# More sevens in the feed-forward blocks, and four first tiles side by side, in a two-layer hybrid model on one core

## The chip, the core and the metric

The kernel runs on 1 core of one Trainium2 chip. The metric is the device time of one execution in microseconds, the median of several runs. Everything is fp32 at the interface; the kernel must return the reference's result for one sequence of 256 tokens with 2048 features.

## What is computed

Two layers. The first mixes tokens by a gated delta rule (8 heads) and a gated linear recurrence, the second by two kinds of softmax attention (8 heads each). After each mixer stands a feed-forward block (SwiGLU), and each of the four parts adds to the residual h:

```python
D_MODEL, SEQ, DEPTH = 2048, 256, 2
D_FF = 5632

def rmsnorm(x, w):
    return x * rsqrt(mean(x * x, axis=-1, keepdims=True) + 1e-6) * w

def swiglu(hn, w_gate, w_up, w_down):
    return (silu(hn @ w_gate) * (hn @ w_up)) @ w_down

h = x
for layer in range(DEPTH):
    if layer % 2 == 0:
        h = h + gdn_rglru_mixer(rmsnorm(h, ab_norm), ...)      # projections, recurrences, w_out
    else:
        h = h + fox_moba_mixer(rmsnorm(h, cd_norm), ...)       # projections, attention, w_out
    h = h + swiglu(rmsnorm(h, ffn_norm[layer]), w_gate[layer], w_up[layer], w_down[layer])
return rmsnorm(h, final_norm)
```

## The kernel before

**Exact products from a fast format.** Every weight tile comes from HBM as fp32 (`raw`, 128 x 1024). ScalarE rounds it to the fast matmul format (`hi`, `S.copy`), VectorE subtracts (`lo = raw - hi`): function `split`. Activations are held the same way, as a pair in `X` or `hid`. A product is then three matmuls: x_hi by w_hi, x_hi by w_lo, x_lo by w_hi. So each weight tile costs a DMA of 512 KB, a cast on ScalarE, a subtraction on VectorE, and matmuls.

**Stages.** `mixer0`, `ffn(0)`, `mixer1`, `ffn(1)` run one after the other, each mixer and each feed-forward part as a phase with tile pools of its own (`phase`). Pools in a feed-forward phase: `hid` (the hidden pair, one buffer), `fx` (everything else, reached as `mx`). The pools for weights lie outside the phases: `wr` (3 buffers, raw), `wh` (4, hi), `wl` (3, lo); in a feed-forward phase four more raw buffers (`raw4`) take four of every seven loads. PSUM has two pools of four banks: `acc` and `msp` (tiles by `ms`).

**Feed-forward.** `ffn` cuts the 5632 hidden features into 11 blocks of 512, in pieces of 4, 4 and 3. A gate/up block (`block` with 4 groups) multiplies X with 512 columns of w_gate and of w_up; both have 2048 rows, four groups of 512. After a piece, two down blocks multiply its `hid` with w_down (4 or 3 groups each) and add to h. In `block`, a plain group is four weight tiles, each for both halves of the tokens: 48 matmuls of 512 columns. A group in `comb` is taken by sevens, as in Strassen's scheme: the 2 x 2 products of (token halves) x (tile pairs) are made from seven products of sums. `combine` makes the sums of the activations (`comb`, on VectorE and ScalarE), `total` those of the weights: a sum T on VectorE, its cast thi on ScalarE, its remainder tlo on VectorE. Seven products of 6 matmuls make 42. `ends` joins the four extra banks M with the banks F: four VectorE operations and a copy on ScalarE, and where F is used (SiLU and product, or adding to h) four more VectorE operations take part. `seven` yields after each product, and `block` deals these steps out between the plain tiles from tile `lead` on. Which groups go by sevens is set in `ffn`: in gate/up block b it is one for b = 0 and for odd b, else two; in a down block always one (`ch`, combined from hid).

`turn` transposes a finished block's activations into `hid` (4 matmuls, a copy, a subtraction); it runs as a hook ahead of a numbered tile of the next block, one half of the tokens at a time, at tiles 2 and 3. Other hooks make `combine(X...)`, `rstd` (the norm's factor, from sums of squares in `ssp`) and `combine(hid...)`.

**The start of mixer0.** `first` (L205) brings xt, the transposed input, in four quarters of 4 k (128 features each), and with each quarter half of three weight tiles; for each it makes X (ScalarE, VectorE), the splits, and 3 tiles x 4 k x 3 matmuls of 256 columns. Then `wstat` takes the other tiles one by one (two loads of 128 x 1024 each, 16 matmuls of 512 columns by hi, 16 of 256 by lo), into a bank of `acc`. Six matmuls on zeros (`Pz`) run ahead. After the first of these tiles, x is loaded into h in four parts, and `sumsq` squares it on ScalarE with a sum; `rstd` follows, and `rstd_rows` after the second tile spreads it over rows (`Prb`). Every finished tile waits for that in its bank, and `convs` then works on two for each new tile.

Each engine works its own list in order; the order between engines comes from semaphores. All loads are issued by SP, in order. Small pieces of the mixers' work are generators, `start`ed and stepped by `tick` after each weight tile.

Of the kernel before, what the change touches and what calls it, by code (L numbers as in the profile page):

```python
# [5 lines left out]
AF = mybir.ActivationFunctionType  # L6
# [4 lines left out]
D = 2048  # L11
# [25 lines left out]
NTAB0 = 152  # L37
# [10 lines left out]
def body(tc, A, out):  # L48
# [13 lines left out]
    mx, ogp = Phase(), Phase()  # L62
# [26 lines left out]
    for _ in range(6):  # L89
        PE.matmul(Pz, wz[:, 128:256], wz[:, 0:256], start=True, stop=True)  # L90
# [91 lines left out]
    def wstat(src, wide=False, mid=None):  # L182
# [5 lines left out]
        P = acc.tile([128, n, T], F32, name="Pw", tag="acc")  # L188
# [16 lines left out]
    def first(srcs, w):  # L205

        xt = ogp.tile([128, NK, T], F32, name="xt", tag="og")
        Ps = [ms([128, T], "Pw") for _ in srcs]
        for q in range(4):
            ks, c = slice(4 * q, 4 * q + 4), slice(q % 2 * 512, q % 2 * 512 + 512)  # L210
            nc.sync.dma_start(xt[:, ks], A["xt"][:, ks])
            if q % 2 == 0:
                ws = [(wr.tile([128, 1024], F32, name="raw"), wh.tile([128, 1024], F32R, name="whi"),
                       wl.tile([128, 1024], F32R, name="wlo")) for _ in srcs]
            for i, (raw, _, _) in enumerate(ws):
                nc.sync.dma_start(raw[:, c], srcs[i][q // 2][:, c])
            if q == 0:
                nc.sync.dma_start(tab[:, 0:NTAB0], A["tab"][:, 0:NTAB0])
                nc.sync.dma_start(col[:, 16:], A["col"][:, 16:])
            for k in range(4 * q, 4 * q + 4):  # L220
# [3 lines left out]
            for P, (raw, hi, lo) in zip(Ps, ws):  # L224
# [3 lines left out]
                for k in range(4 * q, 4 * q + 4):  # L228
# [3 lines left out]
        return Ps  # L232
# [63 lines left out]
    def rstd():  # L296
# [3 lines left out]
        V.tensor_reduce(out=x, in_=ssp, axis=AX.X, op=ALU.add)  # L300
        V.tensor_scalar(out=x, in0=x, scalar1=1.0 / D, scalar2=EPS, op0=ALU.mult, op1=ALU.add)
# [33 lines left out]
    def total(a, b, name):  # L335
# [3 lines left out]
        hi = mx.tile([128, 1024], F32R, name="thi", tag="thi", bufs=2)  # L339
        lo = mx.tile([128, 1024], F32R, name="tlo", tag="tlo", bufs=2)  # L340
# [4 lines left out]
    def combine(x4):  # L345
# [3 lines left out]
        r = mx.tile([128, 2, 4, 2, 128], F32R, name="comb", tag="comb", bufs=3)  # L349
# [22 lines left out]
    def block(src, x, comb, nd, hooks, tail=0, lead=2):  # L372
# [9 lines left out]
        M = [Bank(ms([128, 512], f"M{j}"), ns) for j in range(4)]  # L382
# [62 lines left out]
    def ffn(L, then, fin=None):  # L445
# [4 lines left out]
        def turn():  # L450
            hid, j, t, a = todo.pop(0)
            P = ms([128, 4, 128], "Ph")
            for i in range(4):
                PE.transpose(P[:, i], a[:, i * 128:(i + 1) * 128], tb["ident"])  # L454
            d = hid[:, 4 * j:4 * j + 4, :, t * 128:(t + 1) * 128]
            S.copy(d[:, :, 0], P)
            V.tensor_tensor(out=d[:, :, 1], in0=P, in1=d[:, :, 0].bitcast(F32), op=ALU.subtract)

        b = 0
        for piece in (4, 4, 3):  # L460
            hid = ogp.tile([128, 16, 2, T], F32R, name="hid", tag="hid")
            for j in range(piece):
                hooks = {2: turn, 3: turn} if todo else {}
                if b == 0:
                    hooks[4] = lambda: cx.update({0: combine(X[:, 0:4])})
                    hooks[8] = rstd
                if j == (3 if piece == 4 else 1):
                    hooks[5] = lambda: ch.update({0: combine(hid[:, 0:4])})
                if b == 1:
                    hooks[8] = lambda: cx.update({1: combine(X[:, 4:8])})  # L470
                F, e = block(lambda i, u: gu[b, u, i], lambda k: X[:, k],
# [720 lines left out]
```

## Time and profile before

| | us |
|---|---|
| median of 3 runs | 2254.43 (2252.94 to 2254.56) |
| the profiled execution | 2252.67 |
| its span, first to last instruction | 2250.8 |
| granted TensorE clock | 0.999 |
| TensorE busy in the span | 2232.4 (99%) |
| VectorE busy | 1881.8 (84%) |
| ScalarE busy | 1253.1 (56%) |
| first feed-forward part, first to last matmul | 437.2 to about 1138 |
| second one | 1539.5 to 2241 |

PE is TensorE, PEld its weight loads, DVE VectorE, ACT ScalarE, SP the engine that issues the loads. A row of a group gives the busy time, the mean of one in ns, the idle time of its engine just ahead of it and what ended it. A row of waits names the waiting engine and line, then what it waited for: us in total, times, the longest.

### The profile page before, as it was taken

What the parts mean: (1) busy time and instruction counts of PE and PEld (TensorE: products, weight loads), DVE (VectorE), ACT (ScalarE), POOL (GpSimd) and SP (SyncE); (2) the same over time, 40 slices, a digit from 0 to 9 for tenths busy, and PEclk for the clock granted to TensorE, in tenths of its full rate; (3) what the DMA queues carried; (4) which work ended last, traced back from release to release, by engine and by line L of the source; (5) the groups of instructions that cost most, each with busy time, mean ns of one, the idle gap of its engine ahead of it and who ended that gap; (6) DMA issues with size and microseconds to landing.
All of it is one profiled execution on the core that took longest, in us unless ns stands there. A gap on an engine that the chain in (4) does not pass through costs nothing.

```text
span 2250.8 us, 30139 instructions
## 1 busy us (share of the span) xinstructions
PE 2232.4 (99%) x11070; PEld 1862.6 (83%) x11070; DVE 1881.8 (84%) x2681; ACT 1253.1 (56%) x1663; POOL 2.0 (0%) x6
## 2 busy tenths in 40 slices
PE   8999999999999999999999999999999999999998
PEld 7888888888888888888878888887888888888886
DVE  7899676699979998899976658858998898988998
ACT  7876764565545554455644444445565455555564
POOL 0000000000000000000000000000000000000000
PEclk9999999999999999999999999999999999999999
DMA  7454455666666666666555455556666666566563
GB/s 254 143 175 153 145 155 179 209 211 196 204 199 197 200 193 196 202 199 203 172 153 169 150 170 176 165 184 213 204 196 197 202 205 203 189 202 206 193 218 122
DMA packets 118643, 422.29 MB, mean 188 GB/s; under 512 B 13248, under 2 KB 14784, under 8 KB 118368
## 3 DMA queue, kind: packets, MB, share of 16 engines
q1 hardware_dynamic: 118208, 419.84, 58.7%
q8 instruction: 87, 1.43, 0.3%
q14 instruction: 60, 0.49, 0.1%
q10 hardware_dynamic: 288, 0.52, 0.1%
HBM read 418.22 MB, written 2.10 MB: 187 GB/s over the span
## 4 chain that ended last, share of the span: by engine, by line
PE 95%; DVE 2%; DMA 2%; ACT 0%; issue 0%; SPq 0%; DVEq 0%; ACTq 0%
PE F L368 17%; PE F L369 17%; PE F L367 17%; PE Pw L194 11%; PE Pw L199 5%; PE Px L268 4%; PE Px L269 4%; PE Px L270 4%; PE M L368 4%; PE M L369 4%; PE M L367 3%; PE Ph L454 1%; DMA raw<-in_w0w 1%; DVE wlo L175 1%; PE Psc L997 1%; PE Pt L291 0%
## 5 line engine op out<-in xcount | busy, mean ns | idle before, releaser
L174 ACT CAST whi<-raw 128x1024 fp32r<-128x1024 f32 x734 | 770.9, 1051 | 752.5 <-PE F L369 360.7
L175 DVE TENSOR_TENSOR wlo<-raw,whi 128x1024 fp32r<-128x1024 f32 x734 | 890.2, 1221 | 208.6 <-PE Px L269 67.2
L194 PE MATMUL Pw<-X,whi 128*128 128x512 f32 x1104 | 397.0, 402 | 0.9 <-ACT whi L174 0.9
L367 PE MATMUL F<-whi,X 128*128 128x512 f32 x960 | 375.8, 392 | 0.0
L368 PE MATMUL F<-wlo,X 128*128 128x512 f32 x960 | 374.1, 390 | 0.3 <-DVE wlo L175 0.3
L369 PE MATMUL F<-whi,X 128*128 128x512 f32 x960 | 373.7, 389 | 0.0
L199 PE MATMUL Pw<-X,wlo 128*128 128x256 f32 x1104 | 309.1, 280 | 2.1 <-DVE wlo L175 2.1
L342 DVE TENSOR_TENSOR tlo<-T,thi 128x1024 fp32r<-128x1024 f32 x176 | 214.5, 1222 | 44.2 <-ACT thi L341 43.6
L194 PEld LDWEIGHTS Pw<-X,whi 128*128 128x128 f32 x1104 | 207.2, 188 | 49.9 <-ACT whi L174 1.1
L341 ACT CAST thi<-T 128x1024 fp32r<-128x1024 f32 x176 | 185.1, 1052 | 103.8 <-DVE T L338 80.0
L368 PEld LDWEIGHTS F<-wlo,X 128*128 128x128 f32 x960 | 180.3, 188 | 37.6 <-DVE wlo L175 1.2
L369 PEld LDWEIGHTS F<-whi,X 128*128 128x128 f32 x960 | 180.2, 188 | 37.6
L199 PEld LDWEIGHTS Pw<-X,wlo 128*128 128x128 f32 x1104 | 208.4, 189 | 3.3 <-DVE wlo L175 2.8
L367 PEld LDWEIGHTS F<-whi,X 128*128 128x128 f32 x960 | 180.2, 188 | 36.6
L367 PE MATMUL F<-whi,hid 128*128 128x512 f32 x536 | 209.9, 392 | 0.0
L369 PE MATMUL F<-whi,hid 128*128 128x512 f32 x536 | 208.8, 390 | 0.0
L368 PE MATMUL F<-wlo,hid 128*128 128x512 f32 x536 | 208.7, 389 | 0.0
L369 PEld LDWEIGHTS F<-whi,hid 128*128 128x128 f32 x536 | 100.6, 188 | 21.0
L368 PEld LDWEIGHTS F<-wlo,hid 128*128 128x128 f32 x536 | 100.7, 188 | 20.5
L367 PEld LDWEIGHTS F<-whi,hid 128*128 128x128 f32 x536 | 100.6, 188 | 20.4
L338 DVE TENSOR_TENSOR T<-raw,raw 128x1024 f32<-128x1024 f32 x74 | 90.4, 1223 | 28.0 <-DMA raw<-in_dn 19.0
L338 DVE TENSOR_TENSOR T<-T,raw 128x1024 f32<-128x1024 f32 x88 | 107.5, 1222 | 3.8 <-DMA raw<-in_dn 3.3
(371 smaller groups left out, 3126.2 us busy)
## 6 DMA issues: line engine op xcount, KB each, us to landing
raw<-in_gu SPq DMA_DIRECT2D x352, 512.0 KB, 4.0
raw<-in_dn SPq DMA_DIRECT2D x176, 512.0 KB, 4.2
raw<-in_w0w SPq DMA_DIRECT2D x74, 512.0 KB, 3.7
raw<-in_wo SPq DMA_DIRECT2D x64, 512.0 KB, 3.6
raw<-in_w1w SPq DMA_DIRECT2D x64, 512.0 KB, 3.6
raw<-in_w1x SPq DMA_DIRECT2D x32, 512.0 KB, 3.7
raw<-in_w0x SPq DMA_DIRECT2D x16, 512.0 KB, 3.6
raw<-in_w0w SPq DMA_DIRECT2D x12, 256.0 KB, 5.2
```

The source lines that it names most:

```text
L174: S.copy(hi, raw)
L175: V.tensor_sub(lo, raw, hi.bitcast(F32))
L194: PE.matmul(P.rearrange("p a b -> p (a b)"), hi[:, kk], X[:, k].rearrange("p a b -> p (a b)"), start=k == 0, stop=False)
L199: PE.matmul(P[:, 0], lo[:, kk], X[:, k, 0], start=False, stop=k == NK - 1)
L268: PE.matmul(Ps[t], x[:, 0, ts], hi[:, kk], start=k == 0, stop=False)
L269: PE.matmul(Ps[t], x[:, 0, ts], lo[:, kk], start=False, stop=False)
L338: V.tensor_tensor(out=t, in0=a, in1=b, op=ALU.add)
L341: S.copy(hi, t)
L342: V.tensor_sub(lo, t, hi.bitcast(F32))
L367: PE.matmul(self.t, xh, hi[:, kk], start=self.i == kk == 0, stop=False)
L368: PE.matmul(self.t, xh, lo[:, kk], start=False, stop=False)
L369: PE.matmul(self.t, xl, hi[:, kk], start=False, stop=kk == 1 and self.i == self.n - 1)
```

## The change

1. In `ffn`, the number of groups by sevens is written out for each gate/up block: 0, 2, 2, 2 in the first piece, 2, 2, 2, 2 in the second, 2, 2, 2 in the third. Down blocks keep one. A block without sevens has no M banks and no `ends`; its F go straight to SiLU and product. `combine(hid)` moves from the last gate/up block of a piece to the first down block after it, whose `lead` becomes 5; in the last piece it stays in the second gate/up block. `combine(X...)` is done twice in the first block (tiles 5 and 10).
2. `turn` takes both halves at one hook (tile 2): eight transposes, then the copies and subtractions.
3. A pool `fp` of its own, in the feed-forward phases, for thi, tlo, comb and fa.
4. `first` takes four tiles in pieces of 2, 2, 4, 4 and 4 k, into `acc`; the fourth tile's raw lies in h and `rawb`, its lo in `lob`. The squares are taken in place in xt, and the task `squares` adds them and sums them over features by two one-column matmuls; `rstd` takes the result from PSUM. x is loaded into h behind the ninth to twelfth of the following tiles in the program; in the order of SP's list its four loads stand behind the third, sixth, seventh and ninth weight load that follows `first`. The next three tiles go to `msp` (`spare`). The first load of tables is 280 columns instead of 152, and `Pz` has five matmuls.

The diff, cut to its core:

```diff
-NTAB0 = 152
+NTAB0 = 280
...
+        if not mixer:
+
+            fp.pool = sub("fp", 1)
...
-    for _ in range(6):
+    for _ in range(5):
...
-    def wstat(src, wide=False, mid=None):
+    def wstat(src, wide=False, mid=None, spare=False):
...
-        P = acc.tile([128, n, T], F32, name="Pw", tag="acc")
+        P = ms([128, n, T], "Pw") if spare else acc.tile([128, n, T], F32, name="Pw", tag="acc")
...
     def first(srcs, w):
         xt = ogp.tile([128, NK, T], F32, name="xt", tag="og")
-        Ps = [ms([128, T], "Pw") for _ in srcs]
-        for q in range(4):
-            ks, c = slice(4 * q, 4 * q + 4), slice(q % 2 * 512, q % 2 * 512 + 512)
+        rawb = ogp.tile([128, 4, 1024], F32, name="rawb", tag="og")
+        lob = ogp.tile([128, 4, 1024], F32R, name="lob", tag="og")
+        Ps = [acc.tile([128, T], F32, name="Pw", tag="acc") for _ in srcs]
+        for k0, k1 in ((0, 2), (2, 4), (4, 8), (8, 12), (12, 16)):
+            v, ks, c = k0 // 8, slice(k0, k1), slice(k0 % 8 * 128, k0 % 8 * 128 + (k1 - k0) * 128)
             nc.sync.dma_start(xt[:, ks], A["xt"][:, ks])
...
+            if k0 == 0:
+                raws = [wr.tile([128, 1024], F32, name="raw") for _ in range(3)] + [h[:, 1, 0:1024]]
+            elif k0 == 8:
+                raws = [rawb[:, i] for i in range(4)]
+            if k0 % 8 == 0:
+                his = [wh.tile([128, 1024], F32R, name="whi") for _ in srcs]
+                los = [wl.tile([128, 1024], F32R, name="wlo") for _ in range(3)] + [lob[:, v]]
+            for raw, src in zip(raws, srcs):
+                nc.sync.dma_start(raw[:, c], src[v][:, c])
...
+            if k0 % 4 == 0 and k1 > 2:
+                S.activation(xt[:, ks], xt[:, ks], AF.Square)
+            elif k0 == 2:
+                S.activation(xt[:, 0:4], xt[:, 0:4], AF.Square)
+        return Ps, xt
+
+    def squares(sq):
+        add = lambda a, b: V.tensor_tensor(out=sq[:, a], in0=sq[:, a], in1=sq[:, b], op=ALU.add)
+        add(slice(0, 4), slice(4, 8))
+        add(slice(8, 12), slice(12, 16))
+        yield
+        for a, n in ((8, 4), (2, 2), (1, 1)):
+            add(slice(0, n), slice(a, a + n))
+        yield
+        P = ms([128, 2], "Prs")
+        for t in range(2):
+            PE.matmul(P[:, t:t + 1], sq[:, 0, t * 128:(t + 1) * 128], tb["ones"][:, 0:1], start=True, stop=True)
+        rstd(P)
...
-        hi = mx.tile([128, 1024], F32R, name="thi", tag="thi", bufs=2)
-        lo = mx.tile([128, 1024], F32R, name="tlo", tag="tlo", bufs=2)
+        hi = fp.tile([128, 1024], F32R, name="thi", tag="thi", bufs=2)
+        lo = fp.tile([128, 1024], F32R, name="tlo", tag="tlo", bufs=2)
...
-        for piece in (4, 4, 3):
+        for groups in ((0, 2, 2, 2), (2, 2, 2, 2), (2, 2, 2)):
+            piece = len(groups)
             hid = ogp.tile([128, 16, 2, T], F32R, name="hid", tag="hid")
+            late = {4: lambda hid=hid: ch.update({0: combine(hid[:, 0:4])})}
             for j in range(piece):
-                hooks = {2: turn, 3: turn} if todo else {}
+                hooks = {2: turn} if todo else {}
                 if b == 0:
-                    hooks[4] = lambda: cx.update({0: combine(X[:, 0:4])})
+                    hooks[5] = lambda: cx.update({0: combine(X[:, 0:4])})
                     hooks[8] = rstd
-                if j == (3 if piece == 4 else 1):
-                    hooks[5] = lambda: ch.update({0: combine(hid[:, 0:4])})
-                if b == 1:
-                    hooks[8] = lambda: cx.update({1: combine(X[:, 4:8])})
-                F, e = block(lambda i, u: gu[b, u, i], lambda k: X[:, k],
-                             {m: lambda m=m: cx[m] for m in range(2 - b % 2 if b else 1)}, 4, hooks, lead=2 if b else 5)
+                    hooks[10] = lambda: cx.update({1: combine(X[:, 4:8])})
+                if j == 1 and piece == 3:
+                    hooks.update(late)
+                F, e = block(lambda i, u: gu[b, u, i], lambda k: X[:, k], {m: lambda m=m: cx[m] for m in range(groups[j])}, 4, hooks)
...
-                             {2: turn, 3: turn} if todo else {}, 3 if end and fin else 0)
+                hooks = {2: turn} if todo else {}
+                if p == 0 and piece == 4:
+                    hooks.update(late)
+                F, e = block(lambda i, u: dn[2 * p + i, u0 + u], lambda k: hid[:, k], {0: lambda: ch[0]}, piece, hooks,
+                             3 if end and fin else 0, 5 if 4 in hooks else 2)
...
-        for n, o in enumerate(order[3:]):
-            waiting.append((*o, wstat(tile_of(*o), True, mid=ready if n == 1 else None)))
+        start(squares(sq), 1)
+        for n, o in enumerate(order[4:]):
+            waiting.append((*o, wstat(tile_of(*o), True, mid=ready if n == 1 else None, spare=n < 3)))
             if n == 0:
-                for g in range(4):
-                    nc.sync.dma_start(h[:, :, g * 512:(g + 1) * 512], A["x"][:, :, g * 512:(g + 1) * 512])
-                    sumsq(g)
                 nc.sync.dma_start(tab[:, NTAB0:], A["tab"][:, NTAB0:])
-                rstd()
                 start(lru_rate())
                 continue
+            if n >= 8 and n < 12:
+
+                nc.sync.dma_start(h[:, :, (n - 8) * 512:(n - 7) * 512], A["x"][:, :, (n - 8) * 512:(n - 7) * 512])
```

More of the change, by code (lines that the diff above doesn't have):

```diff
@@ L223, in first @@
                                        op0=ALU.mult, op1=ALU.subtract)
-            for P, (raw, hi, lo) in zip(Ps, ws):
+            for P, raw, hi, lo in zip(Ps, raws, his, los):
                 S.copy(hi[:, c], raw[:, c])
@@ L227, in first @@
                 hi, lo = (t.rearrange("p (k n) -> p k n", n=128) for t in (hi, lo))
-                for k in range(4 * q, 4 * q + 4):
+                for k in range(k0, k1):
                     PE.matmul(P, hi[:, k % 8], X[:, k, 0], start=k == 0, stop=False)
@@ L381, in block @@
              for t in range(2)]
-        M = [Bank(ms([128, 512], f"M{j}"), ns) for j in range(4)]
+        M = [Bank(ms([128, 512], f"M{j}"), ns) for j in range(4)] if ns else []
         def xs(k, t):
@@ L450, in turn @@
         def turn():
[L451 to L457, printed above, removed]
+            Ps = []
+            for hid, j, t, a in todo:
+                P = ms([128, 4, 128], "Ph")
+                for i in range(4):
+                    PE.transpose(P[:, i], a[:, i * 128:(i + 1) * 128], tb["ident"])
+                Ps.append((P, hid[:, 4 * j:4 * j + 4, :, t * 128:(t + 1) * 128]))
```

45 lines of the change are left out of this document (23 added, 22 removed).

## The prediction

> **What bounds the kernel now.** The page comes first: the engines' totals and the shares of the chain that ended last.
>
> ```profile
> span 2250.8 us, 30139 instructions
> PE 2232.4 (99%) x11070; PEld 1862.6 (83%) x11070; DVE 1881.8 (84%) x2681; ACT 1253.1 (56%) x1663; POOL 2.0 (0%) x6
> PE 95%; DVE 2%; DMA 2%; ACT 0%; issue 0%; SPq 0%; DVEq 0%; ACTq 0%
> ```
>
> TensorE carries 95% of the chain, so its work is the time, except where another engine leaves it waiting. VectorE at 84% is the next in line. A matmul's busy time overlaps that of its neighbours, so its price is the distance of two starts, from the timeline of TensorE:
>
> ```profile
> 455.87 0.39 PE L367 MATMUL M<-thi,comb 128*128 128x512 f32 x1
> ...
> 457.23 0.39 PE L367 MATMUL F<-whi,comb 128*128 128x512 f32 x1
> ```
>
> Six steps in 1.36 us: 0.2267 us for a 512-column matmul. With it I read the stages, one feed-forward block each (columns: stretch, length, then busy us of PE, PEld, DVE, ACT, POOL with counts, clock, DMA share, GB/s):
>
> ```profile
> 437.17:481.04 43.87, 43.72 (x196) 35.47 (x194) 41.03 (x58) 26.27 (x32) 0.00 (x0) 1.00 0.75 238
> 652.24:694.40 42.16, 42.16 (x187) 34.91 (x186) 37.48 (x39) 20.70 (x21) 0.00 (x0) 1.00 0.66 213
> 735.52:778.60 43.08, 43.08 (x195) 35.69 (x194) 37.86 (x39) 23.41 (x25) 0.00 (x0) 1.00 0.63 207
> 778.60:820.36 41.76, 41.76 (x190) 34.50 (x188) 38.56 (x40) 24.76 (x26) 0.00 (x0) 1.00 0.60 190
> 1032.84:1074.56 41.72, 41.72 (x189) 34.50 (x188) 39.84 (x41) 24.76 (x26) 0.00 (x0) 1.00 0.60 191
> 1539.45:1584.59 45.14, 44.16 (x196) 35.38 (x194) 41.01 (x57) 26.27 (x32) 0.00 (x0) 1.00 0.71 231
> ```
>
> The second row is a down block: 186 matmuls, 186 x 0.2267 = 42.16 us, exactly its length. The third is a gate/up block with one group by sevens: 186 matmuls and 8 transposes, 43.08, so the transposes take 0.92. The fourth and fifth are blocks with two groups (180 matmuls and 8 transposes): 41.7. In all of these TensorE never waits. Only the first block of each feed-forward part (first and last row) is longer than its 42.16 us of matmuls: by 1.71 and 2.98 us.
>
> **The groups by sevens.** Before, the eleven gate/up blocks of a layer have 1, 1, 2, 1, 2, 1, 2, 1, 2, 1, 2 groups, 16 in all; after, 0 and ten times 2, 20. A plain group is 4 weight tiles x 2 token halves x 6 matmuls = 48, one by sevens 7 x 6 = 42. So 4 groups x 6 x 2 layers = 48 matmuls go: 48 x 0.2267 = **10.9 us off TensorE**.
>
> On VectorE a plain group is 4 subtractions, one by sevens 3 subtractions, 4 sums T and 4 subtractions tlo: 7 more. Its price is again the distance of starts, from its timeline in the fifth row's block:
>
> ```profile
> 1035.24 2.36 DVE L175 TENSOR_TENSOR wlo<-raw,whi 128x1024 fp32r<-128x1024 f32 x2
> 1037.52 1.23 DVE L338 TENSOR_TENSOR T<-T,raw 128x1024 f32<-128x1024 f32 x1
> 1038.65 2.36 DVE L175 TENSOR_TENSOR wlo<-raw,whi 128x1024 fp32r<-128x1024 f32 x2
> 1040.92 1.23 DVE L338 TENSOR_TENSOR T<-T,raw 128x1024 f32<-128x1024 f32 x1
> 1042.05 1.23 DVE L338 TENSOR_TENSOR T<-raw,raw 128x1024 f32<-128x1024 f32 x1
> 1043.19 1.23 DVE L342 TENSOR_TENSOR tlo<-T,thi 128x1024 fp32r<-128x1024 f32 x1
> 1044.32 0.70 DVE L457 TENSOR_TENSOR hid<-Ph,hid 128x512 fp32r<-128x512 f32 x1
> ...
> 1060.99 1.23 DVE L175 TENSOR_TENSOR wlo<-raw,whi 128x1024 fp32r<-128x1024 f32 x1 [0.37 <-issue]
> 1063.65 1.23 DVE L342 TENSOR_TENSOR tlo<-T,thi 128x1024 fp32r<-128x1024 f32 x1 [1.43 <-ACT thi L341]
> ...
> 1074.15 1.30 DVE L480 TENSOR_TENSOR e<-F,e 128x512 f32<-128x512 f32 x2
> 1075.37 1.41 DVE L481 SCALAR_TENSOR_TENSOR fa<-e,rs,fa 128x512 f32<-128x512 f32 x2
> 1076.70 2.35 DVE L175 TENSOR_TENSOR wlo<-raw,whi 128x1024 fp32r<-128x1024 f32 x2
> ```
>
> Eight wide operations from 1035.24 to 1044.32: 1.135 us each. Two narrow ones in 1.22: 0.61 each; two of L481 in 1.33: 0.665 each. A block with two groups has 8 + 6 = 14 wlo, 8 T and 8 tlo, 30 wide operations, 34.05 us; 10 narrow ones (four ends, four around the SiLU, two hid), 6.10; two of L481, 1.33: **41.5 us of VectorE against 41.76 of TensorE**. With one group it is 23 wide operations, 33.5 against 43.08. Before, each block of two stood between lighter ones, and VectorE did part of its T and tlo in advance: the fifth row shows 39.84 busy. After, three, four and three such blocks stand in a row, each with 0.3 us to spare. That is the step on which all depends: every wait of VectorE there that does not overlap a full buffer goes to TensorE.
>
> How much such waiting is there? From the waits of VectorE in the fourth row's block, and the fifth's:
>
> ```profile
> DVE tlo L342 <- ACT thi L341: 2.8, 4, 1.4
> DVE wlo L175 <- issue: 0.4, 1, 0.4
> ...
> DVE tlo L342 <- ACT thi L341: 1.4, 1, 1.4
> DVE wlo L175 <- issue: 0.4, 1, 0.4
> ```
>
> So 1.8 to 3.2 us a block at most. But the fifth row's block has its two waits at 1060.99 and 1063.65, and so none in the 26 us before, while VectorE catches up after the ends of the block ahead; they come when it is ahead itself: ScalarE takes its casts in order, and a thi stands behind a whi that waits for TensorE to give back one of four buffers. A VectorE that is behind pays little of it. Bounds: 0 and 3.2 us a block; I take **0.8**, near the stretch without waits. Against 0.3 to spare, 0.5 us a block is lost, 1.5 to 2 us by the end of a run. Ahead of each run stand a block of no groups or down blocks (23 wide and about 12 narrow, near 34 against 42.16), from which VectorE comes with up to three wlo done, worth 12 x 0.2267 = 2.7 us of TensorE each; the block's end (12 narrow ones, 7.4 us) eats most, and I leave a cushion of 2 us a run (an estimate). So TensorE loses little: **+2.5 us** over the six runs; at 3.2 a block it is 20 x 2.9 - 12 = +46. The combine of hid (one more burst of small operations) moves into the down block, which has 8 us to spare, or into the last run's second block, at the cushion's cost.
>
> The Trainium skill speaks against this step: VectorE: DVE Perf Modes, section "The DRAIN you can't avoid", says that after every operation the pipe must empty before the next starts, and that this can't be skipped. The trace doesn't bear it out: the recorded 1.23 us are paid as 1.135. What the kernel would do if operations never overlapped is a rival below.
>
> The new first block has 192 matmuls and no sevens, so on VectorE 16 wide operations, two combines, the norm's small ones and two of L481, some 30 us against 43.5. The waits of the first and last row above end at wlo behind the T of an early group; this cover replaces them. The six matmuls more are in the count above. **-4.0 us** of the 4.69 (bounds 0 and 4.69). The pool for thi, tlo, comb and fa changes where they lie and which earlier tiles they wait for at a phase's start; no row shows a wait of that kind: 0, bounds ±0.5.
>
> **The first tiles.** The start, in the timelines of ScalarE and TensorE and in the waits of TensorE up to 40 us:
>
> ```profile
> 6.20 1.70 ACT L221 ACTIVATE X<-xt,col 128x256 fp32r<-128x256 f32 x4 [3.98 <-DMA xt<-in_xt]
> 7.81 1.65 ACT L225 CAST whi<-raw 128x512 fp32r<-128x512 f32 x3
> 8.46 0.39 PE L229 MATMUL Pw<-X,whi 128*128 128x256 f32 x1 [1.24 <-ACT whi L225]
> ...
> PE Pw L229 <- ACT whi L225: 1.2, 1, 1.2
> PE Pw L199 <- DVE wlo L175: 1.1, 2, 0.8
> PE Prb L312 <- PE Pw L199: 0.9, 1, 0.9
> PE Pw L194 <- ACT whi L174: 0.9, 1, 0.9
> ...
> h<-in_x SPq DMA_DIRECT2D x4, 512.0 KB, 7.0
> ```
>
> (The last row, of the DMA issues up to 45 us, has the loads of x.) The first piece now has two k instead of four: two of the 0.40 us steps on ScalarE and about 0.2 of the cast fall away, and the first xt is half as long, which may bring its landing forward by up to 0.8. First matmul near 7.0 instead of 8.46: **-1.4** (bounds -0.6 and -1.9; the five dummy matmuls end ahead of it). The other three waits, 2.9 us, stand at the change from narrow to wide tiles, where the four loads of x stood ahead of the next weights in SP's queue, and at Prb, behind a norm that waited for x and for eight Square passes. After, x goes behind later weight tiles in that queue, the squares are taken from xt while four tiles (23 us of matmuls) run, and the first three wide tiles have banks of their own; what queues behind x now are weight loads with two tiles of lead. Of the 2.9 I take 2.3 as saved, as the short second piece may leave a new wait: **-2.3** (bounds +1 and -2.9). The fourth tile as narrow matmuls and two one-column matmuls for the sums add **+0.4**; the four Squares on ScalarE and five sums on VectorE lie beside the 23 us.
>
> **Sum**, on the profiled execution's 2252.67 us (span 2250.8): -10.9 - 4.0 - 1.4 - 2.3 + 0.4 + 2.5 = -15.7, so 2237.0. The median of the runs lies 1.8 higher, at 2254.43: **2238.8 us**, 0.7% faster. What measuring can tell from no change is 0.2%, 4.5 us.
>
> **Rivals.** (1) *VectorE becomes the bound, slower.* If each of the 20 blocks of two keeps the 3.2 us of the fourth row's waits, its VectorE takes 44.7 us, 2.9 more than TensorE; 58 less the cushions' 12 is +46 in place of +2.5: 2282 us. It decides from where 20 (w - 0.3) - 12 eats the gain of 18.2: w = 1.8 us a block. For it: the 1.8 and 3.2 measured. Against: they fall where VectorE is ahead. Chance 0.13. (2) *Operations that never overlap*: 30 x 1.23 + 10 x 0.69 + 2 x 0.75 = 45.3 a block, 3.5 over: 70 - 12 = +58, 2294 us. The starts above are against it. This is the mechanism of the page named in the groups' part. Chance 0.02. (3) *Half eaten*: w near 1.5 costs 12 us, 2248; or with w = 1.8 no change, 2254. For it: any order in which a tlo follows its T too closely. Chance 0.18, of which 0.07 within 0.2%. (4) *The start gains nothing* because four tiles need more bytes before matmuls can run than three: -3.3 falls away, 2242; it lies in the forecast's range. The forecast, with (4), has 0.67.
>
> Faster by over 0.2%: 0.67 + 0.11 = 0.78; within: 0.07; slower: 0.15. The range: below, all bounds of start and first blocks and no loss on VectorE, 2231; above, up to no change, 2255; outside lie (1), (2) and little else.
>
> **What would show it.** Right: 48 fewer 512-column matmuls; blocks of two groups at 41.7 to 42.3 us throughout, their VectorE busy 40 or more; the first blocks at 43.5 without PE waits; first matmul near 7 us and under 1 us of TensorE's waits from there to 40. Wrong: PE waits on tlo or wlo growing from the first to the last block of a run (rival 1), VectorE's starts a full 1.22 apart (rival 2), or DMA waits of whi in the first 30 us (rival 4).

## The result, and the profile after

The changed kernel takes 2242.61 us (median of 6 runs, 2240.28 to 2244.34) against 2253.68 us for the kernel before (6 runs beside it, 2251.65 to 2257.03): ratio 0.9953, 95% interval 0.9942 to 0.9964. It is faster by 11.1 us. The forecast was 2238.8, in a range of 2231 to 2255. The profiled execution of after took 2244.34 us, the slowest of its six; its span is 8.2 us shorter than that of before.

The page's head, engine totals and shares of the chain, after:

```profile
span 2242.6 us, 30180 instructions
PE 2223.1 (99%) x11040; PEld 1856.0 (83%) x11040; DVE 1931.7 (86%) x2730; ACT 1273.8 (57%) x1678; POOL 2.1 (0%) x6
PE 97%; DMA 1%; DVE 1%; ACT 0%; issue 0%; SPq 0%; DVEq 0%; ACTq 0%
```

TensorE still carries the chain. VectorE's busy time grew by 49.9 us and TensorE's fell by 9.3. The same table of stages as for before (stretch, length, then busy us of PE, PEld, DVE, ACT, POOL with counts, clock, DMA share, GB/s):

```profile
436.76:481.30 44.54, 44.54 (x202) 36.74 (x201) 36.06 (x53) 25.67 (x31) 0.00 (x0) 1.00 0.72 243
650.80:692.96 42.16, 42.16 (x187) 34.91 (x186) 36.46 (x38) 21.35 (x21) 0.00 (x0) 1.00 0.65 209
733.76:776.42 42.66, 42.03 (x189) 34.53 (x188) 41.36 (x43) 25.45 (x28) 0.00 (x0) 1.00 0.60 198
776.42:818.17 41.75, 41.75 (x190) 34.61 (x188) 40.90 (x42) 24.79 (x27) 0.00 (x0) 1.00 0.61 198
1027.88:1069.98 42.10, 42.10 (x189) 34.41 (x188) 41.09 (x42) 25.34 (x27) 0.00 (x0) 1.00 0.59 188
1534.83:1579.37 44.54, 44.54 (x201) 36.74 (x200) 36.30 (x54) 25.68 (x31) 0.00 (x0) 1.00 0.72 246
```

The first and last rows are the first blocks of the two feed-forward parts, now equal. The second is a down block, as before. The third is the second block of two groups in its run: 1 us too long. The fourth, a block of two groups further on in the same run, is at its 41.75. The fifth stands at the end of the last run. The waits of TensorE in the first feed-forward part, and of VectorE in the third row's block (total, times, longest):

```profile
PE F L400 <- DVE tlo L374: 1.5, 2, 0.9
```

```profile
DVE T L370 <- DMA raw<-in_gu: 1.0, 1, 1.0
DVE e L516 <- PE F L401: 0.2, 1, 0.2
```

TensorE waits for tlo there. In the third row's block VectorE has no wait for thi; its longest is for a load, ahead of a sum T, so it is late there by a load and not only for want of time.

The start has a new hole. In the timeline:

```profile
12.84 0.28 PE L243 MATMUL Pw<-X,lob 128*128 128x256 f32 x1
12.86 1.70 ACT L233 ACTIVATE X<-xt,col 128x256 fp32r<-128x256 f32 x4 [1.30 <-DMA xt<-in_xt]
14.47 1.64 ACT L237 CAST whi<-raw 128x512 fp32r<-128x512 f32 x3
15.13 0.39 PE L241 MATMUL Pw<-X,whi 128*128 128x256 f32 x1 [2.01 <-ACT whi L237]
```

and the window behind it, with the clock:

```profile
16.00:20.00 4.00, 4.00 (x24) 4.00 (x23) 3.90 (x7) 3.76 (x9) 0.00 (x0) 0.58 1.05 404
20.00:24.00 4.00, 4.00 (x36) 4.00 (x35) 2.92 (x6) 3.19 (x6) 0.00 (x0) 1.00 1.04 394
```

The third piece of xt lands late, TensorE waits 2.01 us, and then runs 24 matmuls in 4 us instead of 36: the granted clock is 0.58. The end, from the last matmul (first row before, second after) to the spans' ends at 2250.8 and 2242.6:

```profile
2240.86 0.39 PE L369 MATMUL F<-whi,hid 128*128 128x512 f32 x1
```

```profile
2231.16 0.39 PE L401 MATMUL F<-whi,hid 128*128 128x512 f32 x1
```

It takes 11.44 us instead of 9.94. All terms, from the starts of the parts in the two traces:

| | forecast | profiled execution |
|---|---|---|
| 48 matmuls fewer | -10.9 | -10.9 (count) |
| first blocks (43.87 and 45.14 before, 44.54 twice after, six matmuls more each) | -4.0 | -2.6 |
| rest of the blocks of two groups | +2.5 | +4.1 |
| start of mixer0, up to the first feed-forward matmul (437.17, now 436.76) | -3.3 | -0.4 |
| last block and the end behind it | 0 | +1.7 |
| mixer1 | 0 | -0.1 |
| sum | -15.7 | -8.2 |

The third term is what is left of the two feed-forward parts, which are 4.10 and 5.32 us shorter (their last down block apart), once the first two terms are taken off.

### The profile page after: what moved, and what is told of

Read it like the earlier page. It is cut to its first block, busy times and chain, and to the rows that moved or that the text cites. A ratio compares the mean times of both kernels' runs of the same rounds, so it can differ in the third digit from the quotient of the medians.

```text
span 2242.6 us, 30180 instructions
## 1 busy us (share of the span) xinstructions
PE 2223.1 (99%) x11040; PEld 1856.0 (83%) x11040; DVE 1931.7 (86%) x2730; ACT 1273.8 (57%) x1678; POOL 2.1 (0%) x6
## 4 chain that ended last, share of the span: by engine, by line
PE 97%; DMA 1%; DVE 1%; ACT 0%; issue 0%; SPq 0%; DVEq 0%; ACTq 0%
PE F L400 16%; PE F L401 16%; PE F L399 16%; PE Pw L197 11%; PE Pw L202 6%; PE Px L298 5%; PE Px L299 4%; PE Px L300 4%; PE M L399 4%; PE M L400 4%; PE M L401 4%; PE Ph L487 1%; DMA raw<-in_gu 1%; PE Psc L1038 1%; PE Pt L321 0%; PE Ps L552 0%
## 5 line engine op out<-in xcount | busy, mean ns | idle before, releaser
L399 PE MATMUL F<-whi,X 128*128 128x512 f32 x848 | 330.5, 391 | 0.0
L400 PE MATMUL F<-wlo,X 128*128 128x512 f32 x848 | 330.4, 390 | 0.0
L401 PE MATMUL F<-whi,X 128*128 128x512 f32 x848 | 330.2, 389 | 0.0
L373 ACT CAST thi<-T 128x1024 fp32r<-128x1024 f32 x208 | 219.1, 1054 | 103.5 <-DVE T L370 73.5
L374 DVE TENSOR_TENSOR tlo<-T,thi 128x1024 fp32r<-128x1024 f32 x208 | 252.7, 1220 | 25.9 <-ACT thi L373 25.3
L401 PEld LDWEIGHTS F<-whi,X 128*128 128x128 f32 x848 | 159.2, 188 | 33.1
L399 PEld LDWEIGHTS F<-whi,X 128*128 128x128 f32 x848 | 159.2, 188 | 32.9
L400 PEld LDWEIGHTS F<-wlo,X 128*128 128x128 f32 x848 | 159.2, 188 | 32.5
L370 DVE TENSOR_TENSOR T<-raw,raw 128x1024 f32<-128x1024 f32 x98 | 119.5, 1220 | 11.1 <-DMA raw<-in_gu 10.5
L370 DVE TENSOR_TENSOR T<-T,raw 128x1024 f32<-128x1024 f32 x104 | 126.8, 1219 | 1.3 <-DMA raw<-in_dn 1.0
L400 PE MATMUL M<-tlo,comb 128*128 128x512 f32 x312 | 121.7, 390 | 0.0
L401 PE MATMUL M<-thi,comb 128*128 128x512 f32 x312 | 121.5, 389 | 0.0
L399 PE MATMUL M<-thi,comb 128*128 128x512 f32 x312 | 121.0, 391 | 0.0
```

The costliest lines, as they stand in the source:

```text
L370: V.tensor_tensor(out=t, in0=a, in1=b, op=ALU.add)
L373: S.copy(hi, t)
L374: V.tensor_sub(lo, t, hi.bitcast(F32))
L399: PE.matmul(self.t, xh, hi[:, kk], start=self.i == kk == 0, stop=False)
L400: PE.matmul(self.t, xh, lo[:, kk], start=False, stop=False)
L401: PE.matmul(self.t, xl, hi[:, kk], start=False, stop=kk == 1 and self.i == self.n - 1)
```

## The experiments

Each time is a median of 4 to 11 runs with the kernel before beside it. On the changed kernel's base they are to be held against 2242.61 (2240.28 to 2244.34), so differences of under about 1.5 us say little.

### The parts alone

`e1_ffn` is before with parts 1 to 3 of the change, `e2_start` before with part 4.

> The kernel before with parts 1 to 3 of the change (groups, turn, own pool) and the old start. By the prediction's sum this is -10.9 - 4.0 + 2.5 = -12.4 us against before; by the trace of after (the two feed-forward parts 4.10 and 5.32 us shorter) it is -9.4. If these parts gave only as much as 8 us, the start would have had to give the other 3.

> The kernel before with part 4 alone (the first tiles, the squares, the late loads of x). By the prediction's sum -3.3 us; by the trace of after -0.4, because a new stall of 2.0 us near 13 us and the 3.4 us at half clock behind it eat a first matmul that is 2.4 us earlier. The profile should then show the same two: a wait of TensorE for whi of 2 us and a granted clock under 0.7 between 16 and 20 us. If the clock stays at 1.0 here, the half clock is a matter of the single execution.

Measured: 2246.76 (2245.57 to 2247.68) and 2250.30 (2248.82 to 2252.39), against 2254.40: -7.6 (ratio 0.9965, 0.9952 to 0.9977) and -4.1 (0.9982, 0.9973 to 0.9991). Together -11.7: the parts add up. The start is worth what was forecast, and the feed-forward blocks less: the -7.6 is the -9.4 of the two parts in the trace of after together with its +1.7 for the last block and the end, which the expectation left out. In the start alone TensorE's clock did not drop:

```profile
PE Pw L238 <- ACT whi L234: 1.3, 2, 1.1
```

```profile
16.00:20.00 4.00, 4.00 (x35) 4.00 (x35) 3.73 (x8) 4.00 (x10) 0.00 (x0) 1.00 1.06 405
```

With the same code the wait was 1.1 us instead of 2.01, the clock stayed at 1.00, and the first feed-forward matmul came at 434.51 instead of 436.76. So the 0.4 us of the profiled execution is that of an unlucky one, and the trace's -0.4 in the expectation was wrong as a price of this part. How often the clock drops in the other executions is not known.

### The start

`e3_tables_later` moves one load group, `e11_xt_by_act` also takes three loads of xt to ScalarE's queue:

```diff
-            if k0 == 2:
+            if k0 == 4:
                 nc.sync.dma_start(tab[:, 0:NTAB0], A["tab"][:, 0:NTAB0])
                 nc.sync.dma_start(col[:, 16:], A["col"][:, 16:])
```

```diff
+        for ks in (slice(0, 2), slice(2, 4), slice(4, 8)):
+            nc.scalar.dma_start(xt[:, ks], A["xt"][:, ks])
         for k0, k1 in ((0, 2), (2, 4), (4, 8), (8, 12), (12, 16)):
...
-            nc.sync.dma_start(xt[:, ks], A["xt"][:, ks])
+            if k0 >= 8:
+                nc.sync.dma_start(xt[:, ks], A["xt"][:, ks])
```

> The kernel after, with the first load of tables and of col issued behind the third piece's loads instead of the second's. Theory: the third piece of xt lands late because SP issues eight small weight loads and the tables ahead of it, one per 0.45 us; two issues fewer ahead of it bring it forward by about 0.9 us and some bytes, so the stall of 2.0 us shrinks to about 1 or less, and if the half clock hangs on that stall it goes too: -1 to -3.7 us against after. Rival: what counts is the bytes that must land before the third piece, the same total as before; then the stall comes back a piece later and the time is that of after, within 0.5.

> The kernel with the tables later, and in addition the first three pieces of xt issued by ScalarE ahead of its first work instead of by SP between the weight loads. Theory (the third piece of xt is late since SP issues one load per 0.45 us and it stands ninth or later in that row): the wait of 1.9 us for whi near 13 us shrinks under 0.8, the granted clock stays at 1.0 behind it, and the time falls by 2 to 3.5 us against that kernel, to about 2238. Rival (the bytes that must land limit it, whoever issues them): the first matmul starts later or the wait moves to the next piece, and the time stays within 1 us of 2240.8.

Measured: 2240.84 (2239.32 to 2242.53) and 2242.51 (2240.43 to 2244.41). In the first the wait was 1.9 us and the clock dropped as in after, and the 1.8 us by which its median is lower lies within the spread. ScalarE began on the third piece at 12.04 us instead of 12.86; but with the loads in the order of after it began at 11.84 in `e2_start` and at 12.51 in `e13_all_64`, so this can't be put down to the two loads. The stall a piece later, which the rival forecast, is not in the trace either: neither of the two is shown. In the second the wait near 13 us was gone in the profile (its two largest waits up to 40 us, and the window):

```profile
PE Pw L246 <- DVE wlo L241: 0.5, 1, 0.5
```

```profile
16.00:20.00 4.00, 4.00 (x35) 4.00 (x35) 4.00 (x8) 3.49 (x8) 0.00 (x0) 1.00 1.05 404
```

and its first feed-forward matmul came at 433.96, 1.7 us ahead of `e3_tables_later`. But the profiled execution is the fastest of its five, and the median gained nothing. That SP's order of issue makes the wait is shown for one execution, not for the time; what the other four ran into stays open.

### Where the small tiles lie

`e4_one_pool` undoes part 3 of the change:

```diff
-            fp.pool = sub("fp", 1)
-        mx.pool = sub("mx" if mixer else "fx", 1)
+            pass
+        fp.pool = mx.pool = sub("mx" if mixer else "fx", 1)
```

> The kernel after with thi, tlo, comb and fa back in the pool of the other small tiles (part 3 undone). The prediction put this at 0 with bounds of 0.5 either way; so the time of after. Rival: the own pool lets thi and comb start without waiting for tiles of the mixer's end, or keeps the wide reads of TensorE away from the small tiles' buffers; then the first blocks of each feed-forward part are longer by 0.5 to 2 us each and nothing else changes.

Measured: 2249.86 (2247.38 to 2250.97), 7.3 us more than after. Neither expectation holds. The first blocks are as in after (44.54); the blocks with sevens are longer (but for the second of a run, whose wait for a load varies), and TensorE has no wait in them. The last block of the second piece, with two groups, in after and here, then a down block here (42.17 in after):

```profile
818.17:859.86 41.69, 41.69 (x189) 34.61 (x188) 41.49 (x45) 24.29 (x26) 0.00 (x0) 1.00 0.63 204
```

```profile
817.58:859.63 42.05, 42.05 (x189) 34.62 (x188) 41.48 (x45) 24.32 (x26) 0.00 (x0) 1.00 0.68 202
902.86:945.21 42.35, 42.35 (x187) 34.92 (x186) 36.79 (x38) 21.33 (x21) 0.00 (x0) 1.00 0.69 211
```

So 0.18 us for each group, and the timeline of TensorE in the down block has it in the matmuls with thi and tlo:

```profile
878.20 0.40 PE L399 MATMUL M<-thi,comb 128*128 128x512 f32 x1
878.44 0.39 PE L400 MATMUL M<-tlo,comb 128*128 128x512 f32 x1
878.66 0.40 PE L401 MATMUL M<-thi,comb 128*128 128x512 f32 x1
878.90 0.39 PE L399 MATMUL M<-thi,comb 128*128 128x512 f32 x1
879.13 0.40 PE L400 MATMUL M<-tlo,comb 128*128 128x512 f32 x1
879.37 0.39 PE L401 MATMUL M<-thi,comb 128*128 128x512 f32 x1
```

Five steps in 1.17 us, 0.234 each instead of 0.227. The program gives the tiles' places in bytes of a partition: thi and tlo begin at 203328 here, at 174272 in after, at 182464 before. Three kernels tested what about the place it is. `e10_raw4_first` is before with raw4's buffers placed first, which lifts thi and tlo to 198848. `e12_fp_128` is after with 128 unused bytes at the head of the own pool; `e13_all_64` has 64 unused bytes behind the constants, which shift nearly everything:

```diff
         todo, cx, ch = [], {}, {}
+        mx.tile([128, 1024], F32, name="raw4", tag="raw4", bufs=4)
```

```diff
             fp.pool = sub("fp", 1)
+            fp.tile([128, 32], F32, name="pad", tag="pad")
```

```diff
     col = cst.tile([128, NCOL], F32, name="col")
+    cst.tile([128, 16], F32, name="pad")
```

> The kernel before with one thing changed: the four buffers raw4 get their place in the pool ahead of all others, so that in the program thi and tlo lie at bytes 198848 to 215232 of a partition instead of 182464 to 198848. No instruction is added. In the kernel with the pool undone, where they lie at 203328 to 219712, each group by sevens took 0.18 us more, in matmuls that read thi or tlo, with no wait. Theory (it is the place that makes TensorE's reads slower): 44 groups x 0.18 = +8 us against before, 2262, matmuls on thi and tlo at 229 to 237 ns from start to start instead of 227, blocks with one group 0.18 and with two 0.36 us longer, the others as before. Rival (sharing a pool with other tiles, or which tile came first, did it): within 1 us of before, since here as in before all share one pool.

> The kernel after with 128 unused bytes a partition at the head of the own pool, so that thi, tlo, comb and fa lie 128 bytes further on (174400 to 190784 for thi and tlo) and nothing else changes but what lies behind them. With raw4 placed first, thi and tlo lay as high as with the pool undone and nothing was slower, so the height in SBUF is out. What is left that sets the slow layout apart: its thi and tlo start at 64 bytes past a multiple of 256, all the others at 192 past one. Theory (TensorE's reads of 512 columns are slower from such a start): 52 groups x 0.18 = 9.4 us as in the slow layout, 7 to 9 us more than after, about 2250, pitches on thi and tlo of 229 to 237 ns. Rival 1 (what counts is the distance of thi from the operand loaded as weights): slower where that is X or hid, 227 ns where it is comb, which moves along; 2 to 4 us. Rival 2 (it was the company of other tiles in that region): the time of after.

> The kernel after with 64 unused bytes a partition behind the constants, so that nearly all that TensorE reads (X, hid, whi, wlo, comb, thi, tlo, h) starts at a multiple of 256 bytes instead of 192 past one. If the start modulo 256 sets the pace of 512-column matmuls, 192 need not be the best: theory: 0 is faster, 1 to 5 ns of 227 for each of 8488 such matmuls, 8 to 40 us less. Rival: 227 ns is what a matmul takes from any start but the slow one, and the time is that of after within 1 us. Third: 0 is a slow start as 64 is, and all 8488 take 4 to 7 ns more, 35 to 60 us.

Measured: `e10_raw4_first` 2254.49 against 2253.57 for before (ratio 1.0001, 0.9993 to 1.0010), its blocks as before: the height is out. `e12_fp_128` 2248.16 (2247.01 to 2249.81), 5.6 us more than after. `e13_all_64` 2239.99 (2239.73 to 2242.28), the time of after within the spread of both. The timeline of `e12_fp_128` decides, since it has quick and slow matmuls side by side (one matmul and the weights loaded beside it, then the first and last of six matmuls each):

```profile
878.58 0.40 PE L402 MATMUL F<-whi,hid 128*128 128x512 f32 x1
878.59 0.19 PEld L400 LDWEIGHTS M<-thi,comb 128*128 128x128 f32 x1
878.82 0.39 PE L400 MATMUL M<-thi,comb 128*128 128x512 f32 x1
...
879.95 0.39 PE L402 MATMUL M<-thi,comb 128*128 128x512 f32 x1
880.18 0.40 PE L400 MATMUL F<-whi,comb 128*128 128x512 f32 x1
...
881.34 0.39 PE L402 MATMUL F<-whi,comb 128*128 128x512 f32 x1
```

thi, tlo and comb were all shifted, and their matmuls take 1.13 / 5 = 0.226 us; whi was not, and with the shifted comb it takes 1.16 / 5 = 0.232, though the same whi with X or hid runs at 0.227. So neither operand's place matters by itself, only the distance of the two. In remainders by 256: thi 64 with comb 192 (`e4_one_pool`) slow; thi 64 with X or hid 192 slow (in `e4_one_pool` and `e12_fp_128`); thi 64 with comb 64 quick; whi 192 with comb 64 slow; all 0 (`e13_all_64`) quick, all 192 (before, after) quick. The first step shows which two tiles meet. While the matmul at 878.58 streams whi (192), the weights of the next one, comb (64), are loaded, and 0.24 us pass to the next start, although whi matches its own weights, hid, and thi matches comb. Over this trace the step from whi or wlo with X or hid to thi with comb takes 0.232 us on average (110 of them; 0.227 in after). The step from whi with X or hid to thi with X or hid takes 0.227 (50 of them): there the next weights match whi, though not thi. So where the tile being streamed and the weights loaded for the next matmul start 128 bytes apart in that sense, a 512-column matmul takes 5 to 7 ns more on average. This is close to the expectation's first rival, which had its price too low: it left out whi with comb and the steps between products. Starts 64 apart were not tried for these tiles.

The Trainium skill, TensorE: Matmul & The Clock Gate, section "Step-by-step: what each phase is for", says that loading the next weights takes no SBUF read bandwidth from the running matmul. At equal remainders the traces agree (0.227 us with a weight load beside each); at 128 bytes' distance the running matmul loses 5 to 7 ns beside such a load, and the traces do not agree. What makes the loss inside the chip is not shown.

### VectorE in the runs of two groups

`e6_alternate` parts the blocks of two by blocks of one, `e7_one_op_more` adds one operation to each:

```diff
-        for groups in ((0, 2, 2, 2), (2, 2, 2, 2), (2, 2, 2)):
+        for groups in ((0, 2, 1, 2), (1, 2, 1, 2), (1, 2, 1)):
```

```diff
                 V.tensor_tensor(out=o, in0=a.t, in1=b, op=op)
+            if ns == 2:
+                V.tensor_tensor(out=w7, in0=M[3].t, in1=w5, op=ALU.add)
```

> The kernel after with one group by sevens instead of two in every second gate/up block (0 2 1 2, 1 2 1 2, 1 2 1: 15 groups a layer instead of 20), so no two blocks of two stand side by side. 10 groups x 6 = 60 matmuls come back: 60 x 0.2267 = 13.6 us. Theory (VectorE's arrears in a run of blocks of two cost TensorE about 4 us, and leave the last block 1.3 us late at the end): these 5 us vanish, so about +8.5 us against after, 2251, no TensorE wait for tlo over 0.5 us in the blocks, and last matmul to end back from 11.4 to 9.9 us. Rival (the waits come from a single block of two, or from the loads, whatever its neighbours; the late end comes from the pool or the order of the last block): the full +13.6, 2256.

> The kernel after with one VectorE operation done twice in each block of two groups (the last sum of its ends, 0.61 us by the prediction's row), 20 in all, 12.2 us of VectorE. Theory (VectorE is the bound within the runs of such blocks: 41.4 of 41.7 us busy): TensorE pays nearly all of it in every block but the first of a run, 14 x 0.6 = 8 to 12 us, 2251 to 2255, with blocks at 42.3 instead of 41.7. Rival (what cost 4 us is the load that T waits for, and VectorE still has slack): 0 to 3 us, under 2246.

Measured: 2252.46 (2250.42 to 2254.66), 9.9 more than after, and 2244.27 (2242.79 to 2247.04), 1.7 more. The 12.2 us of added VectorE work cost TensorE 1.7, little more than the spread: outside the last run VectorE is not the bound of these blocks. Its waits for thi in the first feed-forward part, after and with the added operation, show where it went:

```profile
DVE tlo L374 <- ACT thi L373: 12.7, 16, 1.4
```

```profile
DVE tlo L374 <- ACT thi L373: 7.8, 14, 1.4
```

Then the down block behind the first run, in after and with the added operation, and two more of its blocks, the second of a run and the last one of the last run:

```profile
607.75:650.80 43.05, 43.05 (x195) 35.74 (x194) 39.98 (x44) 23.24 (x24) 0.00 (x0) 1.00 0.61 196
```

```profile
604.61:647.66 43.05, 43.05 (x195) 35.74 (x194) 41.84 (x48) 23.15 (x24) 0.00 (x0) 1.00 0.60 197
730.62:772.39 41.77, 41.77 (x190) 34.53 (x188) 41.22 (x42) 25.05 (x27) 0.00 (x0) 1.00 0.64 201
1024.08:1067.38 43.30, 42.58 (x190) 34.38 (x189) 42.02 (x44) 25.11 (x28) 0.00 (x0) 1.00 0.63 186
```

In the down block VectorE is busy 1.9 us more at the same length: about what the three added operations of the run ahead, 1.8 us, have put off. The four full down blocks are where its waits for thi shrink: 8.3 us of the 12.7 in after, 4.2 of the 7.8 here. The second block even lost its 1 us, with VectorE's wait for the load, and only the last run, which also holds a `combine`, pays.

In `e6_alternate` the time is nearer to the theory's +8.5 us than to the rival's +13.6, but most of the difference is not what the theory said. The two parts grew by 5.6 and 6.5 us of the 13.6 in matmuls, so only some 1.5 us of waiting went, and a single block of two behind a lighter one can have the wait (989.03 to 1031.95: 42.92). There the rival is right. The end is where the theory was right: last matmul at 2242.47, span 2252.9, 10.4 us instead of 11.4. Another 0.7 us is the start of this one execution (first feed-forward matmul at 436.07 instead of 436.76).

`e14_raw8`, on `e13_all_64`, gives the loads an eighth buffer; `e9_T3_pool`, on after, relieves VectorE:

```diff
-        if more and loads[0] > 0 and loads[0] % 7 in (1, 3, 5, 6):
-            raw = mx.tile([128, 1024], F32, name="raw4", tag="raw4", bufs=4)
+        if more and loads[0] > 0 and loads[0] % 8 in (1, 3, 4, 6, 7):
+            raw = mx.tile([128, 1024], F32, name="raw4", tag="raw4", bufs=5)
...
-                a = [fp.tile([128, 512], F32, name=f"fa{t}", tag="fa", bufs=2) for t in range(2)]
+                a = [e[t][0] if e else mx.tile([128, 512], F32, name=f"e{2 * t}", tag=f"e{2 * t}", bufs=1) for t in range(2)]
```

```diff
-        V.tensor_tensor(out=t, in0=a, in1=b, op=ALU.add)
+        (G if name == "T3" else V).tensor_tensor(out=t, in0=a, in1=b, op=ALU.add)
```

> The kernel with everything 64 bytes further on, and an eighth buffer for raw weights: five of every eight loads go to raw4 instead of four of seven, and the SiLU result is written over the sum it is made from, which frees the space of fa. No arithmetic is added. Theory (in the runs of blocks of two it is no shortage of VectorE time that costs TensorE, but T waiting up to 1.4 us for a load that was issued late, since its buffer came free late): VectorE's waits of T for gate/up loads, 5 to 6 us a layer in after, fall to about a third, the second block of each run comes down from 42.3 to 42.9 us to 41.9 or less, and the time falls by 2 to 4 us, to 2236 to 2238. Rival (those waits sit where VectorE is ahead, and without them it is just as late): the time stays at 2240 within 1 us.

> The kernel after with one of the four sums T of each group (T3) on GpSimd instead of VectorE: 52 operations fewer on VectorE, 52 x 1.135 = 59 us. Theory (VectorE's total still counts for the waits at the end of a run and the late end of the kernel, 1.4 us and 1.3 us): 2 to 4 us less than after, 2239 to 2241, if GpSimd makes a sum in the 6.8 us that a step of a group takes at most. Rival (the two engines slow each other while both read two inputs, or T3 comes later than it is wanted): VectorE's operations beside a T3 grow from 1.2 us to 2 or more, and the time grows by 10 us or more.

Measured: 2239.33 (2238.51 to 2240.26) and 2285.58 (2283.47 to 2288.23). The second block of the second run in the base, then with the eighth buffer the same block, the third, and the last of the last run:

```profile
730.89:773.65 42.76, 42.02 (x189) 34.53 (x188) 41.35 (x43) 25.43 (x28) 0.00 (x0) 1.00 0.63 198
```

```profile
732.53:774.32 41.79, 41.79 (x190) 34.54 (x188) 41.49 (x43) 25.88 (x27) 0.00 (x0) 1.00 0.68 202
774.32:816.11 41.79, 41.79 (x189) 34.54 (x188) 41.38 (x42) 25.77 (x27) 0.00 (x0) 1.00 0.66 201
1025.91:1067.75 41.84, 41.84 (x189) 34.54 (x188) 41.28 (x42) 25.59 (x27) 0.00 (x0) 1.00 0.63 191
```

In the base VectorE waits 1.1 us for a load in that block; now the block is at 41.79, without such a wait, though VectorE is as busy: it was the load. VectorE's waits for gate/up loads over the part did not fall to a third (5.7 us instead of 6.2), they are fewer and longer, where VectorE is ahead. The median is 3.3 us below after, and the runs of the two just miss each other (2240.26 and 2240.28). Against its own base, `e13_all_64`, it is 0.7 us, inside the spread, so the time does not show the buffer's worth; the traces do, where the two feed-forward parts are 1.9 and 0.9 us shorter. In its profiled execution the start took that back, with the clock drop (first feed-forward matmul at 436.50 instead of 434.05); whether the other four had it is not known. This is the lowest median: ratio to before 0.9933, 0.9918 to 0.9947.

On GpSimd a T3 does harm. VectorE beside it:

```profile
709.17 1.22 DVE L374 TENSOR_TENSOR tlo<-T,thi 128x1024 fp32r<-128x1024 f32 x1
710.31 4.57 DVE L178 TENSOR_TENSOR wlo<-raw,whi 128x1024 fp32r<-128x1024 f32 x2
710.52 3.28 POOL L370 TENSOR_TENSOR T<-raw,raw 128x1024 f32<-128x1024 f32 x1 [17.70 <-DVE tlo L374]
```

Two VectorE operations that take 2.36 us alone take 4.57 while GpSimd makes one sum: 2.2 us lost for 1.135 saved. The Trainium skill, SBUF — State Buffer, section "SBUF: two separate sides", says that these two engines exclude each other for a whole instruction when VectorE's has two inputs in SBUF and GpSimd's reads SBUF; this row agrees.

## Why the prediction was right, and where it was off

The direction and the range were right, for the reason given: TensorE's matmuls are the time, and 48 fewer of them at 0.2267 us are 10.9 us. The measured 11.1 is little more than that: the other terms, -4.8 us in the forecast, nearly cancelled. The lower end of the range, 2231, does not follow from the bounds that the prediction names, which give about 2234; nothing hangs on it. By its steps:

- **Blocks of two groups.** Those with transposes ran at 41.7 to 42.1 us, as worked out, except the second of the first and second run, at 41.9 to 43.0; from that one on VectorE was 40.9 to 41.7 us busy in each. The loss was 4.1 us instead of 2.5, and some 3.5 of it lie in those four blocks. That the size came near is luck, for the mechanism was not right: the step "every wait of VectorE there that does not overlap a full buffer goes to TensorE", with 0.3 us to spare and a cushion of 2 us a run, made VectorE the next bound. One operation more in each block showed that it can fall further behind and catch up in the down blocks, and an eighth buffer showed that the lost microsecond was a late load. VectorE's waits in the first part's ten blocks of two came to 13 us, 1.3 a block where the prediction took 0.8, and TensorE's own waits in that part to 1.5.
- **First blocks.** -2.6 instead of -4.0. The 1.71 and 2.98 us were length less 186 matmuls, but the rows quoted had 196: eight transposes among them, 0.92 us, were taken for waiting. That step was mis-sized by reading a duration without its count.
- **The start.** -3.3 forecast, -4.1 measured alone. Its two parts were off against each other: the first matmul came 2.4 us earlier (at 6.04) instead of 1.4, the 2.9 us of later waits are gone, and the third piece made a new wait of up to 2.7 us that the sum had only as a bound. The drop of the clock was not foreseen.
- **The own pool.** 0 ± 0.5 was put on the wrong question, waits at a phase's start. Without it the groups and the start would have gained 4.5 us (2249.86 against 2254.40) instead of 11.1. No row of before could show that, since its tiles lay well. That those of after lie well too is luck: nothing in the prediction looks at the bytes where they start.
- **The end.** VectorE's arrears in the last run make the last block 0.24 us and the end 1.5 us longer. The prediction took the last run's cushion as enough; with single blocks there, 1.0 of it came back, and with one VectorE operation more in each block the last block and the end took 1.1 us more still (43.8 instead of 42.7 us from the start of the last down block).
- **Rivals.** (1), VectorE as the bound, fell with the added operation; its point of w = 1.8 us was not reached: the waits were 1.3 us a block of two. (2) fell: in the rows of the kernel with T3 on GpSimd, VectorE's starts at 709.17 and 710.31, ahead of the sum on GpSimd, are 1.14 us apart for a recorded 1.22. The section of the Trainium skill that the prediction names against its step, VectorE: DVE Perf Modes, "The DRAIN you can't avoid", itself adds that a next operation that is not held starts earlier; the prediction left that out. (3) holds in part: 3.8 us of the forecast gain went, but to a load, the first blocks and the end. (4), a start that gains nothing, is what the profiled execution of after shows, and not what the medians show.

## What to carry to other kernels

A block whose second engine is 99% busy by the records need not be bound by it, where lighter blocks follow in which the engine waits less once it comes late: add one operation to each block and see, before counting on either. Where a tile moves between pools, compare the start-to-start time of the matmuls that read it, not only the waits, and, as far as these runs go, keep streamed and weight operands at the same remainder by 256 bytes. Count the instructions in a stretch before calling what is left waiting.

## What the runs showed of the hardware that was not expected

- A matmul of 512 fp32 columns slows from 0.227 to between 0.232 and 0.234 us when the tile that it streams and the weights loaded for the next matmul start 128 bytes apart modulo 256 (`e4_one_pool`, `e12_fp_128`).
- At the end of a wait of TensorE of 1.7 to 2.7 us near 13 us, or up to 1.7 us behind it, the granted clock fell to half for 3.4 us in the profiled executions of six of eight kernels with the new start; with waits of 1.2 us or less it did not in three of three. The six reach the first feed-forward matmul at 435.5 to 436.8, the others at 434.0 to 435.9. The old start shows it too, in two executions with a wait of 2.3 and 2.4 us ahead of the first wide tile (`e1_ffn`, `e10_raw4_first`). The Trainium skill, TensorE: Matmul & The Clock Gate, section "HAM oscillation — how this bites in real kernels", names gaps above about 3.4 us; here shorter ones were enough in some executions.
